# A decoder layer in split float32 on one core: the second norm's rows pipelined on VectorE, three up-projection blocks advancing together over the rows

## The chip, the cores and the metric

One core of a Trainium2 chip runs the kernel: TensorE (PE in the rows) multiplies, VectorE (DVE) and ScalarE (ACT) work element by element, GpSimd (POOL) helps, SyncE (SP) issues the transfers from HBM. The metric is device microseconds of one execution. The times before are the median of 3 runs; the profile is one execution of its own. "Span" is the stretch from the first to the last instruction of that execution.

## What is computed

One layer of a decoder trunk, float32, on 256 positions of 1024 channels. The change lies at the seam of its two halves: the second RMS norm and the ConvFFN behind it.

```
h = rms_norm(x, norm1_g) * (1 + scale1) + shift1
x = x + gate1 * hybrid_token_mixer(h, ...)        # ends in an output projection
h = rms_norm(x, norm2_g) * (1 + scale2) + shift2
u = causal_dwconv(h @ w_up, conv_w, conv_b)       # 1024 -> 2 * 2816, three taps over positions
g, val = split(u, 2)
x = x + gate2 * ((silu(g) * val) @ w_down)        # 2816 -> 1024
```

## The kernel before

**Layout.** Activations are transposed: channels on the 128 partitions, the 256 positions along the free dimension. So the 1024 channels of h are 8 tiles of 128x256, called rows here (`kt` in the code), and a block of 128 output channels is a sum over the 8 rows in half a PSUM bank.

**Split products.** A weight chunk of 128x1024 (512 KB) is split into a rounded part `whi` (L189, ScalarE) and the rest `wlo` (L191, VectorE). An activation is split in the same way, the second norm's h into `h2hi` and `h2lo`. `mm3` (L338 to L340) then gives three matmuls a row: h2hi with whi, h2hi with wlo, h2lo with whi. A block takes 8 rows x 3 = 24 matmuls. A ring of 5 buffers holds split chunks, a ring of 8 the raw ones. SyncE asks for the next raw chunk when its buffer is free (`advance`); `prep` and `get` split ahead of use.

**The second norm (`norm2`, L881).** While the attention part of the output projection ends, the kernel scales each row of x by a gain column `gcol` into `xg` (L870) and sums the squares. The gain is norm2_g (1 + scale2), one 128x1 operation per row (L868). When the sum is there, `rb2` holds 1/rms for each position. Then, for each row, VectorE multiplies y = xg * rb2 into one of three small buffers `hbuf` (L888), ScalarE adds the shift and rounds it into h2hi (L889), and VectorE forms h2lo = y + shift - h2hi (L890). VectorE and ScalarE run this part in the order in which it is written (`manual_schedule`).

**The ConvFFN.** 22 pairs (a gate block and a value block each). Pair 0 is done apart (`up0`): plain float32 matmuls on xg (L919) that don't need the norm, corrected behind it by rb2 (L927, L928). A later pair i is two blocks of 24 matmuls in half-banks of banks 0 to 3 (`up`). Each block gets its convolution: one operation on ScalarE (L903) and two taps on VectorE (L905). The gate goes through Silu (L942, with a load of ScalarE's table the first time), is multiplied by the value (L948), and the product is split (L950, L951). The down-projection (`down`) of pair i - 2 follows pair i; its 8 outputs fill the halves of banks 5, 7, 4 and 6 over all pairs. The order on PE, DVE and ACT outside the norm is set by a scheduler from the program's order and the dependences.

Of the kernel before, what the change touches and what calls it, by code (L numbers as in the profile page):

```python
# [8 lines left out]
F32 = mybir.dt.float32  # L9
F32R = mybir.dt.float32r  # L10
I32 = mybir.dt.int32
AF = mybir.ActivationFunctionType
OP = mybir.AluOpType
AX = mybir.AxisListType

S = 256
D = 1024
KT = D // 128
# [13 lines left out]
V_N2 = 56  # L32
# [15 lines left out]
def mixer_ffn(ctx: ExitStack, tc: tile.TileContext, xT_d, c_d, vec_d, alog_d, ada_d,  # L48
# [7 lines left out]
    act, dve, pool, pe, sp = nc.scalar, nc.vector, nc.gpsimd, nc.tensor, nc.sync  # L56

    def T(shape, name, dt=F32, tag=None):
        return sb.tile(shape, dt, name=name, tag=tag or name)
# [113 lines left out]
    def done(i):  # L173
        freed.add(i)
        advance()
# [20 lines left out]
    def split():  # L196
        for _ in split_steps():
            pass

    def prep(la=LA):  # L200
        while st["split"] < min(st["get"] + 1 + la, NCHUNK):
            split()

    def get(la=LA):
        prep(la)
        i = st["get"]
        st["get"] += 1
        return ready.pop(i)

    cb = T([128, 1024], "cb")  # L210
    vec = T([128, V_ALL], "vec")
    alog = T([128, SH], "alog")
    xT = T([128, KT, S], "xT")
# [17 lines left out]
    mod = T([128, 48], "mod")  # L231
# [20 lines left out]
    def ada_bias(a, b):  # L252
        dve.tensor_tensor(mod[:, a:b], mod[:, a:b], vec[:, V_BADA + a:V_BADA + b], op=OP.add)

    hbuf = Ring(3, [128, S], "hbuf")
# [5 lines left out]
    rb2 = T([128, S], "rb2")  # L261
    acc = T([128, S], "accs")

    def rms_sum(parts, n, pb, between=lambda: None):
        for i, p in enumerate(parts):
            for t in range(2):
                pe.matmul(pb[:, t:t + 1], p[:, t * 128:(t + 1) * 128], ones[:, 0:1], start=(i == t == 0),
                          stop=(i == len(parts) - 1), skip_group_check=True)
        r = rt()
        act.activation(r[:, 2:4], pb[:, 0:2], AF.Sqrt, bias=epsc, scale=1.0 / n)  # L270
        between()
        dve.reciprocal(r[:, 0:2], r[:, 2:4])
        return r
# [15 lines left out]
    def rms_transpose(r, pb):  # L289
        for t in range(2):  # L290
            i = pe.transpose(pb[:, 256 + t * 128:384 + t * 128], r[:, t:t + 1].to_broadcast([128, 128]), ident)
        return i
# [9 lines left out]
    def square_add(i, src, dst, last, late=9):  # L302
        s = dst if i == 0 else sq_r()
        act.activation(s, src, AF.Square)
        if 0 < i < last:
            (dve if i >= late else pool).tensor_tensor(dst, dst, s, op=OP.add)
        return s
# [3 lines left out]
    sc1 = T([128, 2 * KT], "sc1")  # L311
# [25 lines left out]
    def mm3(out, w, h, start, stop):  # L337
        pe.matmul(out, w[0], h[0], start=start, stop=False, skip_group_check=True)  # L338
        pe.matmul(out, w[1], h[0], start=False, stop=False, skip_group_check=True)  # L339
        pe.matmul(out, w[0], h[1], start=False, stop=stop, skip_group_check=True)  # L340

    def sl(w, c):
        return w[0][:, c], w[1][:, c]

    def blk(k):
        return slice(k * 128, k * 128 + 128)


    gcol = T([128, 16], "gcol")
# [4 lines left out]
    def half(b, i):  # L354
        return bank[b][:, i * 256:i * 256 + 256]
# [68 lines left out]
    for kt in range(KT):  # L424
        if kt == 0:
            s1_gain(0)
            s1_h(0)
            ws = [get(0)]
# [15 lines left out]
                                     op0=OP.add, op1=OP.mult)  # L444
            ada_bias(3, 4)
        else:
            s1_mm(kt, [ws[0]], final[:8])
            ws.append(get(0))
            if kt == 2:
# [3 lines left out]
                                         op1=OP.mult)  # L453
# [3 lines left out]
        if kt < KT - 1:  # L457
            s1_h(kt + 1)
            ws = [get(0)]
# [294 lines left out]
    k = P["qk"]  # L754
# [27 lines left out]
    def side(u):  # L782
        for f, a in at.pop(u, []):
            f(*a)
# [3 lines left out]
    for i in range(5):  # L788
        if P["zi"]:
            with tc.issue_after(X["z2"].ins):  # L790
                w = get()
        else:
            w = get()
# [11 lines left out]
    for j in range(6):  # L805
        m, hf = divmod(j, 2)
        bs = (bank[4], bank[6]) if j % 2 else (bank[5], bank[7])
        for q4 in range(4):
            w = get()
            side(5 + 4 * j + q4)  # L810
            c = st["get"] - 1
            for k2 in range(2):
                kt = q4 * 2 + k2 + (m == 2)
# [22 lines left out]
    def aacc(d):  # L836
        return half((0, 1, 5, 4, 6, 7, 2, 3)[d], 0)
# [5 lines left out]
    for d in range(8):  # L843
        w = get()
# [9 lines left out]
    xg = h32  # L854
    for d in range(8):
        w = get()
        if d == 6:
            prep(5)
        side(37 + d)
        for kt in range(8):  # L860
            mm3(aacc(d), sl(w, blk(kt)), (X["ahi"][:, kt], X["alo"][:, kt]), start=(kt == 0), stop=(kt == 7))
        for e in {0: (), 1: (0, 1)}.get(d, (d,)):
            t = hbuf()
            dve.tensor_tensor(t, aacc(e), rb, op=OP.mult)
            dve.scalar_tensor_tensor(xT[:, e], t, gate1(e), xT[:, e], op0=OP.mult, op1=OP.add)
            tail.append(square_add(e, xT[:, e], acc, P['n2l'], P['sqa']))
            g = gcol[:, 8 + e:9 + e]
            dve.scalar_tensor_tensor(g, mod[:, 24 + e:25 + e], sc1[:, KT + e:KT + e + 1], vec[:, V_N2 + e:V_N2 + e + 1],  # L868
                                     op0=OP.add, op1=OP.mult)
            act.activation(xg[:, e, 0:S], xT[:, e], AF.Copy, scale=g)  # L870
        if d == 5:
            tc.keep_in_program_order(act.activation(warm, epsc, AF.Sqrt))
        if d == 6:
            ada_bias(32, 40)
            act.activation(xg[:, :, S:], mod[:, 32:40].unsqueeze(2).to_broadcast([128, KT, 2]), AF.Copy)
    prep()
    assert not at, at
    h2hi = T([128, KT, S], "h2hi", F32R, tag="big_qT")
    h2lo = T([128, KT, S], "h2lo", F32R, tag="big_kT")

    def norm2():  # L881
        r2 = rms_sum([acc] + tail[P['n2l']:], D, bank[5])
        with tc.manual_schedule(engines={mybir.EngineType.DVE, mybir.EngineType.Activation}):
            rms_transpose(r2, bank[5])
            act.activation(rb2, bank[5][:, 256:512], AF.Copy)
            for kt in range(KT):
                y, shift = hbuf(), mod[:, 32 + kt:33 + kt]
                dve.tensor_tensor(y, xg[:, kt, 0:S], rb2, op=OP.mult)  # L888
                act.activation(h2hi[:, kt], y, AF.Identity, bias=shift)  # L889
                dve.scalar_tensor_tensor(h2lo[:, kt], y, shift, h2hi[:, kt].bitcast(F32), op0=OP.add, op1=OP.subtract)  # L890


    fbuf = T([128, 8, S], "fbuf", tag="big_v")
# [7 lines left out]
    def fconv(a, i, src):  # L901
        w = V_FW + 3 * i
        act.activation(a, src, AF.Identity, bias=vec[:, V_FB + i:V_FB + i + 1], scale=vec[:, w + 2:w + 3])  # L903
        for s in (1, 2):
            dve.scalar_tensor_tensor(a[:, s:], src[:, :S - s], vec[:, w + 2 - s:w + 3 - s], a[:, s:],  # L905
                                     op0=OP.mult, op1=OP.add)
# [6 lines left out]
    def up0():  # L913

        ws = get(), get()
        ps = bank[0][:, 0:S + 2], bank[1][:, 0:S + 2]
        for kt in range(KT):
            for p, w in zip(ps, ws):
                pe.matmul(p, w[:, blk(kt)], xg[:, kt], start=(kt == 0), stop=(kt == KT - 1), skip_group_check=True)  # L919
            if kt == P['n2']:  # L920
                norm2()
        for j in (2, 1):
            done(st["get"] - j)
        u = []
        for j in range(2):
            t = hbuf()
            dve.tensor_tensor(t, ps[j][:, 0:S], rb2, op=OP.mult)  # L927
            dve.tensor_scalar(t, t, ps[j][:, S:S + 1], None, op0=OP.add)  # L928
            u.append(t)
        return u  # L930

    def up(i):
        g, v = cg_r(), cv2_r()
        if i == 0:
            pg, pv_ = up0()
        else:
            pg, pv_ = half(2 * i % 4, 0), half((2 * i + 1) % 4, 0)
            w = get()
            for kt in range(KT):
                mm3(pg, sl(w, blk(kt)), (h2hi[:, kt], h2lo[:, kt]), start=(kt == 0), stop=(kt == KT - 1))  # L940
        fconv(g, i, pg)
        act.activation(g, g, AF.Silu)  # L942
        if i:
            w = get()
            for kt in range(KT):
                mm3(pv_, sl(w, blk(kt)), (h2hi[:, kt], h2lo[:, kt]), start=(kt == 0), stop=(kt == KT - 1))
        fconv(v, NF + i, pv_)
        dve.tensor_tensor(v, v, g, op=OP.mult)  # L948
        fh, fl = fhi_r(), flo_r()
        act.activation(fh, v, AF.Copy)  # L950
        dve.tensor_tensor(fl, v, fh.bitcast(F32), op=OP.subtract)  # L951
        return fh, fl

    fs = {}
    for i in range(NF):
        fs[i] = up(i)
        if i >= LAG:
            down(fs.pop(i - LAG), i == LAG)
        if 8 <= i < 16:
            ada_mul(32 + i)  # L960
        if 9 <= i < 17:
            ada_sum(31 + i)
        if i == 17:
            ada_bias(40, 48)
# [3 lines left out]
    ws = [get(), get()]  # L968
# [79 lines left out]
```

## Time and profile before

| what | value |
|---|---|
| median of 3 runs | 437.0 us (436.76 to 437.31) |
| the profiled execution | 437.12 us |
| its span | 435.4 us |
| TensorE busy | 428.0 us (98%) |
| VectorE busy | 338.7 us (78%) |
| ScalarE busy | 259.0 us (59%) |
| GpSimd busy | 34.6 us (8%) |
| granted TensorE clock, mean | 0.996 |

The profiled execution's own time is 1.72 us above its span and 0.12 above the median. In the rows below, times are microseconds from the start of the span unless a column says ns; L888 is line 888 of the kernel before. A matmul's busy time contains the run through the array, which overlaps the next matmul: the pitch between starts is what one costs in a dense stream. PEld are the weight loads of TensorE.

### The profile page before, as it was taken

How to read it: one execution, taken by the hardware profiler on the slowest of the kernel's cores; microseconds unless marked ns; L12 is line 12 of the kernel's file. 1: busy time of each engine (PE TensorE's matmuls, PEld its weight loads, DVE VectorE, ACT ScalarE, POOL GpSimd, SP SyncE). 2: the span in 40 equal slices, each digit the busy share in tenths (PEclk: the TensorE clock that was granted, in tenths of full speed). 3: DMA queues.
4: the chain of work that ended last, by engine and by line, in shares of the span. 5: the costliest groups of instructions: out<-in, count | busy, mean ns of one | idle time of the engine just before them, and what ended most of it. 6: DMA issues, size and time to landing. Idle time of an engine off the chain costs nothing.

```text
span 435.4 us, 7753 instructions
## 1 busy us (share of the span) xinstructions
PE 428.0 (98%) x2952; PEld 387.7 (89%) x2952; DVE 338.7 (78%) x670; ACT 259.0 (59%) x513; POOL 34.6 (8%) x31
## 2 busy tenths in 40 slices
PE   8999999999999999999999899999999999999996
PEld 9799998768766668888999699999999999999996
DVE  2779968999788998668699489787877876776655
ACT  4365448826998965642258386567766655555540
POOL 2000000000000020201220000032233200000000
PEclk9899999999999999999999999999999999999999
DMA  7999964899277644057790527866776565454002
GB/s 283 400 415 408 394 200 172 306 325 336 74 279 276 219 164 176 17 201 250 294 390 11 230 109 240 296 239 202 278 255 233 204 219 184 169 193 147 2 2 96
DMA packets 29589, 96.71 MB, mean 222 GB/s; under 512 B 3552, under 2 KB 6000, under 8 KB 29552
## 3 DMA queue, kind: packets, MB, share of 16 engines
q1 hardware_dynamic: 29520, 96.20, 61.1%
q8 instruction: 23, 0.38, 0.4%
q14 instruction: 14, 0.11, 0.1%
q10 hardware_dynamic: 32, 0.02, 0.0%
HBM read 95.14 MB, written 1.06 MB: 221 GB/s over the span
## 4 chain that ended last, share of the span: by engine, by line
PE 84%; DVE 7%; ACT 5%; issue 1%; DMA 1%; POOL 1%; ACTq 0%; POOLq 0%
PE bank L338 15%; PE bank L339 15%; PE bank L340 15%; PE bank L847 6%; PE bank L798 4%; PE bank L819 4%; PE bank L821 4%; PE bank L823 3%; PE bank L822 3%; DVE adax L239 2%; PE bank L412 2%; PE bank L228 2%; ACT whi L189 2%; DVE wlo L191 2%; PE bank L919 1%
## 5 line engine op out<-in xcount | busy, mean ns | idle before, releaser
L191 DVE TENSOR_TENSOR wlo<-raw,whi 128x1024 fp32r<-128x1024 f32 (+2 forms) x107 | 132.8, 1242 | 17.8 <-ACT whi L189 17.7
L189 ACT ACTIVATE whi<-raw 128x1024 fp32r<-128x1024 f32 (+2 forms) x106 | 108.6, 1032 | 39.8 <-PE bank L340 23.7
L338 PE MATMUL bank<-h2hi,whi 128*128 128x256 f32 x336 | 95.4, 285 | 2.1 <-ACT h2hi L889 1.9
L339 PE MATMUL bank<-h2hi,wlo 128*128 128x256 f32 x336 | 94.5, 283 | 0.0
L340 PE MATMUL bank<-h2lo,whi 128*128 128x256 f32 x336 | 93.9, 284 | 0.0
L338 PEld LDWEIGHTS bank<-h2hi,whi 128*128 128x128 f32 x336 | 64.4, 192 | 3.7 <-ACT h2hi L889 3.2
L339 PEld LDWEIGHTS bank<-h2hi,wlo 128*128 128x128 f32 x336 | 64.4, 192 | 0.0
L340 PEld LDWEIGHTS bank<-h2lo,whi 128*128 128x128 f32 x336 | 63.8, 192 | 0.2 <-DVE h2lo L890 0.2
L905 DVE SCALAR_TENSOR_TENSOR fbuf<-bank,vec,fbuf 128x255 f32<-128x255 f32 x84 | 40.3, 481 | 29.4 <-ACT fbuf L903 28.1
L244 POOL TENSOR_TENSOR ada<-ada,cb 128x1024 f32<-128x1024 f32 x11 | 28.8, 2621 | 270.2 <-DMA ada<-in_ada_dram 270.2
L338 PE MATMUL bank<-fsp,whi 128*128 128x256 f32 x176 | 49.8, 284 | 0.0
L339 PE MATMUL bank<-fsp,wlo 128*128 128x256 f32 x176 | 49.7, 283 | 0.0
L340 PE MATMUL bank<-fsp,whi 128*128 128x256 f32 x176 | 49.6, 283 | 0.0
L903 ACT ACTIVATE fbuf<-bank,vec 128x256 f32<-128x256 f32 x42 | 23.4, 560 | 36.2 <-PE bank L340 36.2
L239 DVE SCALAR_TENSOR_TENSOR ada<-ada,cb 128x1024 f32<-128x1024 f32 x27 | 32.8, 1216 | 3.0 <-DMA ada<-in_ada_dram 3.0
L338 PEld LDWEIGHTS bank<-fsp,whi 128*128 128x128 f32 x176 | 33.8, 192 | 0.1
L339 PEld LDWEIGHTS bank<-fsp,wlo 128*128 128x128 f32 x176 | 33.8, 192 | 0.0
L340 PEld LDWEIGHTS bank<-fsp,whi 128*128 128x128 f32 x176 | 33.7, 192 | 0.0
L821 PE MATMUL bank<-whi,hhi 128*128 128x512 f32 x70 | 29.5, 422 | 0.0
L847 PE MATMUL bank<-y,raw 128*128 128x256 f32 x128 | 28.9, 380 | 0.0
L822 PE MATMUL bank<-wlo,hhi 128*128 128x512 f32 x70 | 28.6, 408 | 0.0
L823 PE MATMUL bank<-whi,hlo 128*128 128x512 f32 x70 | 28.3, 405 | 0.0
(214 smaller groups left out, 783.1 us busy)
## 6 DMA issues: line engine op xcount, KB each, us to landing
raw<-in_wup_dram SPq DMA_DIRECT2D x44, 512.0 KB, 4.1
ada<-in_ada_dram SPq DMA_DIRECT2D x38, 512.0 KB, 5.1
raw<-in_wdn_dram SPq DMA_DIRECT2D x22, 512.0 KB, 3.6
raw<-in_winq_dram SPq DMA_DIRECT2D x16, 512.0 KB, 4.8
raw<-in_wout_dram SPq DMA_DIRECT2D x16, 512.0 KB, 3.8
adax<-in_ada_dram SPq DMA_DIRECT2D x10, 512.0 KB, 9.6
raw<-in_win_dram SPq DMA_DIRECT2D x8, 456.0 KB, 9.7
raw<-in_win_dram SPq DMA_DIRECT2D x7, 512.0 KB, 9.8
```

What stands on the lines that cost most here:

```text
L189: act.activation(hi[:, c], t[:, c], AF.Copy)
L191: (pool if lo_on_pool(i) else dve).tensor_tensor(lo[:, c], t[:, c], hi[:, c].bitcast(F32), op=OP.subtract)
L239: dve.scalar_tensor_tensor(t, t, 1.0, sc, op0=OP.mult, op1=OP.mult, accum_out=mod[:, i:i + 1])
L244: pool.tensor_tensor(adas[i], adas[i], sc, op=OP.mult)
L338: pe.matmul(out, w[0], h[0], start=start, stop=False, skip_group_check=True)
L339: pe.matmul(out, w[1], h[0], start=False, stop=False, skip_group_check=True)
L340: pe.matmul(out, w[0], h[1], start=False, stop=stop, skip_group_check=True)
L821: pe.matmul(bs[t], hhi[:, kt, blk(t)], w[0][:, wc], start=(q4 == k2 == 0), stop=False)
L822: pe.matmul(bs[t], hhi[:, kt, blk(t)], w[1][:, wc], start=False, stop=False)
L823: pe.matmul(bs[t], hlo[:, kt, blk(t)], w[0][:, wc], start=False, stop=(kt == KT - 1))
L847: pe.matmul(sacc(d), w[:, blk(kt)], X["y32"][:, kt], start=(kt == d % 2 == 0), stop=(kt == 7), skip_group_check=True)
L905: dve.scalar_tensor_tensor(a[:, s:], src[:, :S - s], vec[:, w + 2 - s:w + 3 - s], a[:, s:], op0=OP.mult, op1=OP.add)
```

## The change

Three edits. The gain columns of all 8 rows are formed by two 128x8 operations at the start of the attention output projection's loop, where a 128x1 operation per row stood in the loop. In the norm, y of the next row is written ahead of h2lo of the row before. In `up`, the value block of pair 1 and the gate block of pair 2 are fetched together with the gate block of pair 1, and all three take a row before any takes the next; the gate block of pair 2 sums in bank 6 (it was bank 0). A call of `prep()` is added in `up0`.

```diff
         side(37 + d)
+        if d == 0:
+            g = gcol[:, 8:16]
+            dve.tensor_tensor(g, mod[:, 24:32], sc1[:, KT:], op=OP.add)
+            dve.tensor_tensor(g, g, vec[:, V_N2:V_N2 + 8], op=OP.mult)
...
-            g = gcol[:, 8 + e:9 + e]
-            dve.scalar_tensor_tensor(g, mod[:, 24 + e:25 + e], sc1[:, KT + e:KT + e + 1], vec[:, V_N2 + e:V_N2 + e + 1],
-                                     op0=OP.add, op1=OP.mult)
-            act.activation(xg[:, e, 0:S], xT[:, e], AF.Copy, scale=g)
+            act.activation(xg[:, e, 0:S], xT[:, e], AF.Copy, scale=gcol[:, 8 + e:9 + e])
...
-            for kt in range(KT):
-                y, shift = hbuf(), mod[:, 32 + kt:33 + kt]
-                dve.tensor_tensor(y, xg[:, kt, 0:S], rb2, op=OP.mult)
-                act.activation(h2hi[:, kt], y, AF.Identity, bias=shift)
-                dve.scalar_tensor_tensor(h2lo[:, kt], y, shift, h2hi[:, kt].bitcast(F32), op0=OP.add, op1=OP.subtract)
+            ys = {}
+            for kt in range(KT + 1):
+                if kt < KT:
+                    ys[kt] = hbuf()
+                    dve.tensor_tensor(ys[kt], xg[:, kt, 0:S], rb2, op=OP.mult)
+                    act.activation(h2hi[:, kt], ys[kt], AF.Identity, bias=mod[:, 32 + kt:33 + kt])
+                if kt:
+                    k = kt - 1
+                    dve.scalar_tensor_tensor(h2lo[:, k], ys.pop(k), mod[:, 32 + k:33 + k], h2hi[:, k].bitcast(F32),
+                                             op0=OP.add, op1=OP.subtract)
...
         ws = get(), get()
+        prep()
...
-            w = get()
+            if i == 2:
+                pg = half(6, 0)
+            ws = [] if i == 2 else [(pg, get())]
+            if i == 1:
+                ws += [(pv_, get()), (half(6, 0), get())]
             for kt in range(KT):
-                mm3(pg, sl(w, blk(kt)), (h2hi[:, kt], h2lo[:, kt]), start=(kt == 0), stop=(kt == KT - 1))
+                for p, w in ws:
+                    mm3(p, sl(w, blk(kt)), (h2hi[:, kt], h2lo[:, kt]), start=(kt == 0), stop=(kt == KT - 1))
         fconv(g, i, pg)
         act.activation(g, g, AF.Silu)
-        if i:
+        if i > 1:
             w = get()
```

VectorE's order in the norm, before (L888 is y, L890 is h2lo; hbuf_163 to hbuf_165 are the three buffers):

```order
L272 RECIPROCAL rt_173<-rt_173 128x2
L888 TENSOR_TENSOR hbuf_164<-h_168,rb_175 128x256
L890 SCALAR_TENSOR_TENSOR h2lo<-hbuf_164,mod,h2hi 128x256
L888 TENSOR_TENSOR hbuf_165<-h_168,rb_175 128x256
L890 SCALAR_TENSOR_TENSOR h2lo<-hbuf_165,mod,h2hi 128x256
L888 TENSOR_TENSOR hbuf_163<-h_168,rb_175 128x256
L890 SCALAR_TENSOR_TENSOR h2lo<-hbuf_163,mod,h2hi 128x256
```

The same place in the changed kernel (L891 is y, L895 is h2lo):

```order
L272 RECIPROCAL rt_173<-rt_173 128x2
L891 TENSOR_TENSOR hbuf_164<-h_168,rb_175 128x256
L891 TENSOR_TENSOR hbuf_165<-h_168,rb_175 128x256
L895 SCALAR_TENSOR_TENSOR h2lo<-hbuf_164,mod,h2hi 128x256
L891 TENSOR_TENSOR hbuf_163<-h_168,rb_175 128x256
L895 SCALAR_TENSOR_TENSOR h2lo<-hbuf_165,mod,h2hi 128x256
L891 TENSOR_TENSOR hbuf_164<-h_168,rb_175 128x256
L895 SCALAR_TENSOR_TENSOR h2lo<-hbuf_163,mod,h2hi 128x256
```

One y now stands between a row's y and its h2lo.

TensorE's order over rows 0 and 1, as a difference (bank_67 is bank 2 with pair 1's gate block, bank_68 bank 3 with its value block, bank_71 bank 6 with pair 2's gate block):

```order
 L339 MATMUL bank_68<-h2hi,wlo_89 128x256
 L340 MATMUL bank_68<-h2lo,whi_84 128x256
+L338 MATMUL bank_71<-h2hi,whi_85 128x256
+L339 MATMUL bank_71<-h2hi,wlo_90 128x256
+L340 MATMUL bank_71<-h2lo,whi_85 128x256
 L338 MATMUL bank_67<-h2hi,whi_83 128x256
 L339 MATMUL bank_67<-h2hi,wlo_88 128x256
+L340 MATMUL bank_67<-h2lo,whi_83 128x256
 L338 MATMUL bank_68<-h2hi,whi_84 128x256
 L339 MATMUL bank_68<-h2hi,wlo_89 128x256
-L340 MATMUL bank_67<-h2lo,whi_83 128x256
 L340 MATMUL bank_68<-h2lo,whi_84 128x256
```

Before, a row was 6 matmuls, the two with h2lo last; now it is 9, each block's three together.

ScalarE's order behind the rows in the changed kernel (L909 convolution, L954 Silu with its table load, L962 the rounded product, L189 the split of the next weights; bank_71 is bank 6):

```order
L909 ACTIVATE fbuf<-hbuf_163,vec 128x256
L909 ACTIVATE fbuf<-hbuf_164,vec 128x256
L954 ACT_TABLE_LOAD
L954 ACTIVATE fbuf<-fbuf 128x256
L909 ACTIVATE fbuf<-bank_67,vec 128x256
L909 ACTIVATE fbuf<-bank_68,vec 128x256
L962 ACTIVATE fsp<-fbuf 128x256
L909 ACTIVATE fbuf<-bank_71,vec 128x256
L189 ACTIVATE whi_83<-raw_78 128x1024
```

Before, pair 0's gate convolution stood ahead of the last row's h2hi, and that of bank_67 ahead of the table load.

## Rows read from the trace of the kernel before

**Rows 1.** The page, busy time of TensorE.
```profile
PE 428.0 (98%) x2952; PEld 387.7 (89%) x2952; DVE 338.7 (78%) x670; ACT 259.0 (59%) x513; POOL 34.6 (8%) x31
```

**Rows 2.** Stage windows: length, busy (x) PE PEld DVE ACT POOL, PEclk, DMA share, GB/s.
```profile
242.70:252.00 9.30, 7.28 (x45) 5.80 (x44) 6.35 (x17) 3.66 (x8) 0.00 (x0) 1.00 0.88 343
...
259.00:345.00 86.00, 86.00 (x717) 85.98 (x717) 70.72 (x96) 57.44 (x88) 19.91 (x8) 1.00 0.72 245
345.00:432.00 87.00, 86.95 (x725) 86.75 (x723) 61.67 (x98) 44.26 (x67) 0.00 (x0) 1.00 0.37 122
```

**Rows 3.** Chain of waits, row 0 of the norm: start, length on the chain, what.
```profile
241.74 0.44 DVE hbuf L888
242.20 0.52 ACT h2hi L889
242.74 0.48 DVE h2lo L890
```

**Rows 4.** Timeline of VectorE: start, us, instruction [idle before <- releaser].
```profile
243.14 0.41 DVE L888 TENSOR_TENSOR hbuf<-h,rb 128x256 f32<-128x256 f32 x1
...
250.12 0.42 DVE L888 TENSOR_TENSOR hbuf<-h,rb 128x256 f32<-128x256 f32 x1
250.45 0.42 DVE L927 TENSOR_TENSOR hbuf<-bank,rb 128x256 f32<-128x256 f32 x1
250.91 0.36 DVE L928 TENSOR_SCALAR hbuf<-hbuf,bank 128x256 f32<-128x256 f32 x1
251.18 0.48 DVE L890 SCALAR_TENSOR_TENSOR h2lo<-hbuf,mod,h2hi 128x256 fp32r<-128x256 f32 x1
...
252.64 0.48 DVE L890 SCALAR_TENSOR_TENSOR h2lo<-hbuf,mod,h2hi 128x256 fp32r<-128x256 f32 x1
...
254.31 1.00 DVE L905 SCALAR_TENSOR_TENSOR fbuf<-bank,vec,fbuf 128x255 f32<-128x255 f32 x2 [0.54 <-ACT fbuf L903]
...
260.07 1.21 DVE L191 TENSOR_TENSOR wlo<-raw,whi 128x1024 fp32r<-128x1024 f32 x1
```

**Rows 5.** Waits from 242 to 259 us: who, for whom, us, times, longest.
```profile
PEld bank L338 <- ACT h2hi L889: 3.2, 6, 0.6
```

**Rows 6.** Timeline of TensorE, row 0 and the end of pair 2.
```profile
242.76 0.39 PE L338 MATMUL bank<-h2hi,whi 128*128 128x256 f32 x1
...
243.28 0.39 PE L340 MATMUL bank<-h2lo,whi 128*128 128x256 f32 x1
243.50 0.28 PE L338 MATMUL bank<-h2hi,whi 128*128 128x256 f32 x1
...
258.31 0.28 PE L340 MATMUL bank<-h2lo,whi 128*128 128x256 f32 x1
258.71 0.38 PE L338 MATMUL bank<-h2hi,whi 128*128 128x256 f32 x1
259.02 0.39 PE L338 MATMUL bank<-fsp,whi 128*128 128x256 f32 x1
```

**Rows 7.** Timeline of ScalarE behind the rows.
```profile
254.29 1.28 ACT L942 ACT_TABLE_LOAD   x1
255.59 0.42 ACT L942 ACTIVATE fbuf<-fbuf 128x256 f32<-128x256 f32 x1
255.91 0.59 ACT L903 ACTIVATE fbuf<-hbuf,vec 128x256 f32<-128x256 f32 x1
...
256.71 1.00 ACT L903 ACTIVATE fbuf<-bank,vec 128x256 f32<-128x256 f32 x2
257.61 1.05 ACT L189 ACTIVATE whi<-raw 128x1024 fp32r<-128x1024 f32 x1
```

**Rows 8.** Timeline of SyncE's queue: issues of weight transfers.
```profile
226.07 16.88 SPq L146 DMA_DIRECT2D raw<-in_wup_dram  x2
```

**Rows 9.** The gain columns and the nearest 128x8 operation: ns min/median/max, first and last start.
```profile
L868 DVE SCALAR_TENSOR_TENSOR gcol<-mod,sc,vec x8: 209/214/215, 111.8 to 162.2; 128x1 f32<-128x1 f32 x8
L253 DVE TENSOR_TENSOR mod<-mod,vec x11: 150/151/160, 12.6 to 346.7; 128x1 f32<-128x1 f32 x8, 128x8 f32<-128x8 f32 x3
```

## The prediction

> **What bounds the kernel now.** The busy times come first: TensorE is busy for 428.0 of 435.4 us, so only a place where it idles, or where its stream gets longer, can move the time [rows 1]. The stage windows say where that is. From 242.70 to 252.00 it is busy for 7.28 of 9.30 us, with 45 matmuls; from 259 to 345 for all 86.00, with 717 matmuls, so one each 0.120 us; from 345 to 432 for 86.95 of 87 [rows 2]. The granted clock is 1.00 in all three, so the level is 2.4 GHz throughout and no clock is to be won. The chain of waits shows what the first of these stretches waits for: VectorE's product y (L888), ScalarE's rounding h2hi (L889), VectorE's rest h2lo (L890), and only then the next y [rows 3]. VectorE issues the next y 0.40 us behind the h2lo (242.74 to 243.14), so one of the 8 rows takes 243.14 - 241.74 = 1.40 us [rows 3, 4]. In it TensorE has 6 matmuls, 0.72 us. The weight loads wait 3.2 us for h2hi [rows 5].
>
> How much is lost is read from TensorE's timeline. The four blocks of pairs 1 and 2 are 4 x 24 = 96 matmuls, 11.52 us at 0.120. The first starts at 242.76; the last starts at 258.31 and frees the array at 258.43. That is 15.67 us, so 4.15 are idle. Then two gaps follow: one matmul of pair 3 at 258.71, and the down-projection of pair 0 at 259.02 [rows 6]. Its place in a dense stream would be 259.02 - 0.12 = 258.90.
>
> **The rows, new order.** VectorE runs y0, y1, h2lo0, y2, h2lo1 and so on. A y costs it 0.33 to 0.34 us (250.12 to 250.45), an h2lo 0.40 [rows 3, 4]. The first h2lo can't come sooner: y0 at 241.74, h2hi at 242.20, h2lo at 242.74, as now, with y1 in the gap. From then on h2hi of the next row is ready in time: y(k+1) starts 0.74 us ahead of its h2lo or more, and ScalarE's 0.46 + 0.52 + 0.02 us on the chain overlap one further VectorE pair. So h2lo(k) starts at 242.74 + 0.74k, and row 7 at 247.92, done at 248.40 (0.48 each). Three buffers are enough: y(k+3) overwrites what h2lo(k) has read two instructions ahead. Before, row 7's h2lo starts at 252.64, 9.9 us behind row 0's; now it would be 5.2 us behind it [rows 4].
>
> **Three blocks over the rows.** TensorE gets 9 matmuls a row, 1.08 us, against 0.74 us for a row on VectorE: it becomes the slower of the two and stays dense. Row 0 keeps its stall: two matmuls at 242.76, the third, which needs h2lo, at 243.28, the next at 243.50 [rows 6]. The other 69 of the 72 follow at 0.120: 243.50 + 8.28 = 251.78. The up block of pair 2's value half (24, weights split ahead of the norm) ends at 254.66. So the down-projection starts 258.90 - 254.66 = **4.24 us** sooner. Of 4.15 + 0.47 us of gaps only row 0's 0.38 is left. With the pipelined rows alone, two blocks would have 0.72 us of matmuls a row against 0.74, almost the same; the third block is mainly cover for a late row.
>
> **What must be ready by then.** I follow VectorE and ScalarE behind the rows in the changed order.
> - Pair 0's product. Its four operations on VectorE start at 247.58 (ahead of h2lo7), 248.32, 248.59 and 249.05: 0.34 + 0.40 with h2lo7 between, then 0.27, then 0.46 for one that needs the result before it [rows 4]. ScalarE's convolution of the gate, 0.59, begins when the second is done; the gate's two taps follow at 249.35 and end at 250.35, 1.00 for two [rows 4, 7]. The table load stands behind them: 250.39 to 251.67; Silu 251.69 to 252.11; the product at 252.14 [rows 7]. Meanwhile ScalarE takes the convolutions of banks 2 and 3, 252.01 and 252.45, then the rounded product, 252.90 to 253.31. VectorE's rest comes behind two taps, at 253.43, and ends at 253.85. TensorE needs it for its third matmul, 254.66 + 0.24 = 254.90. Margin 1.05.
> - Bank 6. The third block accumulates there, and the seventh output of the down-projection overwrites it, 18 matmuls in, at 256.82. Its second tap sits behind pair 1's product, that behind Silu, that behind the split of pair 3's weights on ScalarE (0.96 us on the chain at 253.65, 1.05 by itself [rows 7]). It ends at 255.88. Margin 0.94.
> - Pair 3's weights. VectorE's part follows that tap: 255.80 to 257.01 at 1.21 [rows 4]. TensorE's second matmul of pair 3 needs it at 257.66. Margin 0.65, the thinnest. The raw weights were asked for at 226.07 [rows 8].
>
> So I cost the tail at nothing, under the cover of 48 matmuls (5.76 us); if it comes L later, TensorE loses L - 0.65.
>
> The table load took 1.28 us at 254.29 and the next Silu started at 255.59, 1.30 us later: nothing else stands there [rows 7]. The Trainium skill says otherwise (ScalarE: Activation LUTs, What ACT_TABLE_LOAD costs): a switch is the 1283 ns load and about 1380 ns of drain. By that rule the rest of pair 0 would end at 255.23 and cost 0.33, the weights would be another 0.40 late, and the sum would be 3.51 rather than 4.24. The trace disagrees with it here, so the sum keeps the row.
>
> **gcol and prep.** Eight 128x1 operations of 0.21 us at 111.8 to 162.2 go; two 128x8 ones come, 0.15 by the nearest row [rows 9]. Seven of the eight stand between the dependent steps of a reciprocal square root while TensorE is dense, and the two new ones stand there too: I take zero, between a loss of 0.3 (two, if something waited for them) and a gain of 1.7 (eight, if VectorE bound there). The added prep() issues nothing: the splits stand at the same places in the order. No DMA is added; SP's order is unchanged, and transfers are let go by buffers that TensorE's stream frees, so they move with it.
>
> **Sum.** 4.24 us off the profiled execution's 437.12 is 432.9; off the median, 437.0, 432.8. I take **432.8**. From 259 on TensorE never waits, so nothing downstream takes it back by slack.
>
> **Rivals.**
> 1. The tail becomes the bound. For it: margins of 0.65 to 1.05 us rest on some 20 modelled starts. One more piece as long as the table load's 1.28 would cost 1.28 - 0.65 = 0.63, a loss of the same size as the skill's rule gives; 433.4, or up to 434.5 if it is late by 2.3. Chance 0.10.
> 2. The rows don't overlap (a buffer of the ring released late). With 1.40 us a row, TensorE has 1.08 in it; row 7's h2lo is usable at 253.18, its 7 last matmuls end near 254.1, pair 2's value half at 257.0: gain 1.9, 435.1. Against: the order is as told, and the ring's waits are on instructions long done. Chance 0.04.
> 3. Given back later: the weight stream can't come 4 us sooner. For it: the DMA share is 0.72 in 259 to 345 [rows 2]. Against: TensorE didn't wait there once. 437.0, no change. Chance 0.04.
> 4. Slower: bank 6. If the split of pair 3's weights waits for its transfer, Silu, pair 1's product and the tap queue behind it, and TensorE stops in the middle of the down-projection, where before the third block had bank 0. It decides when the transfer lands after 253.65; slower than before it gets where that is over 0.94 + 4.24 = 5.2 us later, past 258.8. At 6 us late it gives 437.0 + 0.8 = 437.8. Against: 27 us of lead [rows 8]. Chance 0.02.
>
> **Numbers.** The forecast has 0.80. The least the time can be is all gaps gone, 0.38 more, 432.4; with the 0.24 by which the lowest run lies under the median, 432.1. The upper end takes rival 1 at a delay of 2 us: 434.2. Faster by over 0.2% (about what a measurement of this kernel can tell from no change): 0.80 + 0.10 + 0.04 = 0.94; within: 0.04; slower: 0.02.
>
> **What would show it.** TensorE's timeline: no idle entry between 243.5 and the end, its down-projection first at about 254.7, nine matmuls each 1.08 us. VectorE: y and h2lo in turn at 0.74 us, no idle entry on h2hi behind the first. ScalarE: its idle entries before h2hi gone. The span is 431.2. Wrong: an idle entry on TensorE for the rounded product, for bank 6's tap or for the weights of pair 3 (rival 1 or 4), rows still at 1.40 (rival 2), or idle entries past 259 (rival 3).

## The result, and the profile after

The changed kernel takes **432.92 us** (median of 6 runs, 432.34 to 434.12), the kernel before 437.06 in the same comparison (6 runs, 436.43 to 437.31). The ratio is 0.9915, with a 95% interval of 0.9904 to 0.9926: faster by 4.1 us. The forecast was 432.8 in a range of 432.1 to 434.2. The profiled execution took 432.34, with a span of 430.6.

The page's busy times of the changed kernel answer to [rows 1]:

```profile
PE 425.2 (99%) x2952; PEld 386.7 (90%) x2952; DVE 339.6 (79%) x664; ACT 258.9 (60%) x513; POOL 34.1 (8%) x31
```

The same 2952 matmuls are in the profile. VectorE has 6 instructions fewer (eight gain columns out, two in). The stage windows of the changed kernel, with the columns of [rows 2], say where the time came from:

```profile
242.70:252.00 9.30, 9.29 (x77) 9.20 (x77) 8.28 (x23) 6.37 (x12) 0.00 (x0) 1.00 0.93 352
252.00:259.00 7.00, 7.00 (x61) 7.00 (x60) 6.95 (x15) 7.00 (x13) 0.00 (x0) 1.00 0.35 122
259.00:345.00 86.00, 86.00 (x719) 86.00 (x718) 72.61 (x95) 56.67 (x88) 19.85 (x8) 1.00 0.73 246
```

In the first stretch 77 matmuls run where 45 ran [rows 2]; 9.30 us at 0.120 is 77.5, so it is dense. From 259 to 345 nothing has changed: 719 matmuls for 717, DMA share 0.73 for 0.72. Nothing was given back there.

VectorE's timeline in the changed kernel (L891 is y, L895 is h2lo, L963 the rest of a pair's product, L911 a convolution tap, L191 VectorE's part of a weight split; "x2" is two records in one row):

```profile
241.27 0.76 DVE L891 TENSOR_TENSOR hbuf<-h,rb 128x256 f32<-128x256 f32 x2 [1.15 <-ACT rb L886]
242.27 0.48 DVE L895 SCALAR_TENSOR_TENSOR h2lo<-hbuf,mod,h2hi 128x256 fp32r<-128x256 f32 x1 [0.24 <-ACT h2hi L892]
242.67 0.42 DVE L891 TENSOR_TENSOR hbuf<-h,rb 128x256 f32<-128x256 f32 x1
243.00 0.48 DVE L895 SCALAR_TENSOR_TENSOR h2lo<-hbuf,mod,h2hi 128x256 fp32r<-128x256 f32 x1
...
247.39 0.47 DVE L895 SCALAR_TENSOR_TENSOR h2lo<-hbuf,mod,h2hi 128x256 fp32r<-128x256 f32 x1
...
252.94 0.41 DVE L963 TENSOR_TENSOR fsp<-fbuf,fsp 128x256 fp32r<-128x256 f32 x1
...
254.90 0.47 DVE L911 SCALAR_TENSOR_TENSOR fbuf<-bank,vec,fbuf 128x254 f32<-128x254 f32 x1
255.29 1.22 DVE L191 TENSOR_TENSOR wlo<-raw,whi 128x1024 fp32r<-128x1024 f32 x1
```

Two y's run ahead of the first h2lo; from then on they take turns, one row in 243.00 - 242.27 = 0.73 us where it was 1.40. Row 7's h2lo starts 247.39 - 242.27 = 5.12 us behind row 0's, where it was 9.9 [rows 4]. The idle entry of 0.24 for h2hi is the only one of its kind.

TensorE's timeline, row 0 and the end of the three blocks, answers to [rows 6]:

```profile
242.29 0.39 PE L338 MATMUL bank<-h2hi,whi 128*128 128x256 f32 x1
242.51 0.28 PE L339 MATMUL bank<-h2hi,wlo 128*128 128x256 f32 x1
242.81 0.39 PE L340 MATMUL bank<-h2lo,whi 128*128 128x256 f32 x1
243.03 0.28 PE L338 MATMUL bank<-h2hi,whi 128*128 128x256 f32 x1
...
254.19 0.28 PE L338 MATMUL bank<-fsp,whi 128*128 128x256 f32 x1
...
254.43 0.28 PE L340 MATMUL bank<-fsp,whi 128*128 128x256 f32 x1
...
257.07 0.28 PE L338 MATMUL bank<-h2hi,whi 128*128 128x256 f32 x1
257.19 0.28 PE L339 MATMUL bank<-h2hi,wlo 128*128 128x256 f32 x1
```

Row 0 still has its stall (242.51 to 242.81). The down-projection starts at 254.19, 11.90 us behind the first matmul of the rows; before it was 259.02 - 242.76 = 16.26, of which 0.12 is the one matmul of pair 3 that stood ahead of it [rows 6]. All waits of the weight loads between 241 and 262 us come to one row of the view of waits, and ScalarE's for y to another:

```profile
ACT h2hi L892 <- DVE hbuf L891: 2.1, 7, 0.5
...
PEld bank L340 <- DVE h2lo L895: 0.2, 1, 0.2
```

The 3.2 us for h2hi [rows 5] are gone.

**A measure that is free of what lies ahead.** In the profiled executions shown here the first matmul of the rows starts anywhere from 242.18 to 243.10, whatever the kernel, before any of this seam has run. So I compare executions by the *stretch* from that matmul to the start of the kernel's last matmul. Before: 431.68 - 242.76 = 188.92. After: 426.87 - 242.29 = 184.58, which is **4.34 shorter**. The span shrank by 435.4 - 430.6 = 4.8; the other 0.47 is where the rows began, 242.29 for 242.76, and is not owed to the change by anything seen here: with the new gain columns the rows begin at 242.18 to 243.10 in seven executions, with the old ones at 242.24 to 242.97 in three.

### The profile page after: what moved, and what is told of

It is laid out like the page before. It is cut to its first block, busy times and chain, and to the rows that moved or that the text cites. A ratio compares the mean times of both kernels' runs of the same rounds, so it can differ in the third digit from the quotient of the medians.

```text
span 430.6 us, 7750 instructions
## 1 busy us (share of the span) xinstructions
PE 425.2 (99%) x2952; PEld 386.7 (90%) x2952; DVE 339.6 (79%) x664; ACT 258.9 (60%) x513; POOL 34.1 (8%) x31
## 4 chain that ended last, share of the span: by engine, by line
PE 87%; DVE 6%; ACT 3%; DMA 1%; issue 1%; POOL 1%; ACTq 0%; POOLq 0%
PE bank L340 16%; PE bank L338 16%; PE bank L339 16%; PE bank L847 6%; PE bank L798 4%; PE bank L819 4%; PE bank L821 4%; PE bank L823 3%; PE bank L822 3%; DVE adax L239 2%; PE bank L412 2%; PE bank L228 2%; PE bank L926 2%; DVE wlo L191 2%; ACT whi L189 1%; DMA ada<-in_ada_dram 1%
## 5 line engine op out<-in xcount | busy, mean ns | idle before, releaser
L191 DVE TENSOR_TENSOR wlo<-raw,whi 128x1024 fp32r<-128x1024 f32 (+2 forms) x107 | 133.1, 1245 | 18.7 <-ACT whi L189 18.7
L189 ACT ACTIVATE whi<-raw 128x1024 fp32r<-128x1024 f32 (+2 forms) x106 | 108.5, 1032 | 40.3 <-PE bank L340 23.6
L340 PE MATMUL bank<-h2lo,whi 128*128 128x256 f32 x336 | 95.2, 283 | 0.0
L911 DVE SCALAR_TENSOR_TENSOR fbuf<-bank,vec,fbuf 128x255 f32<-128x255 f32 (+1 forms) x84 | 40.2, 481 | 26.8 <-ACT fbuf L909 25.5
L909 ACT ACTIVATE fbuf<-bank,vec 128x256 f32<-128x256 f32 x42 | 23.5, 561 | 33.9 <-PE bank L340 33.9
```

What stands on the lines that cost most here:

```text
L189: act.activation(hi[:, c], t[:, c], AF.Copy)
L191: (pool if lo_on_pool(i) else dve).tensor_tensor(lo[:, c], t[:, c], hi[:, c].bitcast(F32), op=OP.subtract)
```

## The experiments

The theory: the time comes from VectorE's serial row alone; TensorE was short of rows, and the third block covers a late row but earns little; everything behind the rows has 0.65 us or more to spare. The rivals: the third block is what pays (more work per row, so that 1.40 us hide); the new tail is what bounds; the gain columns have a share.

**The changed kernel once more**, with no edit, on the chip of the next three kernels, beside 17 runs of the kernel before (437.15, 436.21 to 438.09).

> The changed kernel once more, as the yardstick for the runs beside it. Theory (rows and blocks keep TensorE dense from row 0 on): 4.2 us under the kernel before, one stall of 0.3 us on the first h2lo, no idle entry later. Rival (the gain is that of one chip): less than 3.5 us.

Measured: 432.91 (4 runs, 432.38 to 433.22), ratio 0.9902, interval 0.9887 to 0.9916; stretch 426.91 - 242.33 = 184.58, as in the first profile. The gain stands on a second comparison, and the stretch repeats to 0.01 us.

**Pipelined rows alone.** The gain columns, `up` and `prep()` are as before; the edit to the changed kernel, cut:

```diff
-            if i == 2:
-                pg = half(6, 0)
-            ws = [] if i == 2 else [(pg, get())]
-            if i == 1:
-                ws += [(pv_, get()), (half(6, 0), get())]
+            w = get()
             for kt in range(KT):
-                for p, w in ws:
-                    mm3(p, sl(w, blk(kt)), ...)
+                mm3(pg, sl(w, blk(kt)), ...)
...
-        if i > 1:
+        if i:
```

> The rows pipelined on VectorE, nothing else. Theory (the serial row of 1.40 us was the loss; two blocks have 0.72 us of matmuls against a row of 0.74): 3.6 to 4.2 us under the kernel before, with idle entries of TensorE in the rows of 0.5 us at most together, and up to 0.4 us for pair 0's product, since ScalarE here splits the next weights ahead of the table load. Rival (the third block is what keeps TensorE busy): a gain under 2 us, with idle entries on h2hi or h2lo in every row.

Measured: 432.90 (4 runs, 432.35 to 433.33), ratio 0.9902, interval 0.9887 to 0.9917; stretch 427.76 - 242.97 = 184.79, so 4.13 of the 4.34 us. TensorE's timeline of this kernel, rows 0 and 1 and the start of the down-projection:

```profile
242.97 0.39 PE L338 MATMUL bank<-h2hi,whi 128*128 128x256 f32 x1
...
244.06 0.28 PE L339 MATMUL bank<-h2hi,wlo 128*128 128x256 f32 x1
244.22 0.39 PE L340 MATMUL bank<-h2lo,whi 128*128 128x256 f32 x1
244.44 0.30 PE L338 MATMUL bank<-h2hi,whi 128*128 128x256 f32 x1
...
255.08 0.28 PE L338 MATMUL bank<-fsp,whi 128*128 128x256 f32 x1
```

With six matmuls a row TensorE is about as fast as VectorE and runs into row 1 before its h2lo is there: the next matmul comes 0.16 behind 244.06 where 0.12 is the pitch, and the one after that 0.22. The down-projection starts 12.11 us behind the first matmul, for 11.90 in the change. That is the 0.21 us by which the third block shortens the stretch; the timed medians can't tell the two kernels apart.

**Three blocks alone.** The changed kernel with the norm's loop as it was:

```diff
-            ys = {}
-            for kt in range(KT + 1):
...
+            for kt in range(KT):
+                y, shift = hbuf(), mod[:, 32 + kt:33 + kt]
+                dve.tensor_tensor(y, xg[:, kt, 0:S], rb2, op=OP.mult)
+                act.activation(h2hi[:, kt], y, AF.Identity, bias=shift)
+                dve.scalar_tensor_tensor(h2lo[:, kt], y, shift, h2hi[:, kt].bitcast(F32), ...)
```

> Three blocks over the rows, the rows serial as before (gcol and prep as in the change). Theory: a row stays at 1.40 us, TensorE has 1.08 us of matmuls in it, pair 2's value half would end 1.9 us sooner, and the tail behind the rows (pair 0's product, the next weights) costs 0.3 to 0.8 of that: 1.1 to 1.9 us under the kernel before. Rival (the third block carries the gain): 3 us or more.

Measured: 435.81 (12 runs, 434.96 to 436.76), ratio 0.997, interval 0.9959 to 0.9981; stretch 429.88 - 242.27 = 187.61, so 1.31 shorter than before. The waits of its weight loads from 241 to 262 us:

```profile
PEld bank L338 <- ACT h2hi L890: 1.4, 5, 0.3
PEld bank L338 <- ACT fsp L957: 0.4, 1, 0.4
PEld bank L339 <- DVE wlo L191: 0.2, 1, 0.2
PEld bank L338 <- DVE fbuf L906: 0.2, 1, 0.2
...
```

A row of 1.40 us with 1.08 us of matmuls leaves TensorE waiting for h2hi, as before but less: 1.4 us for 3.2. And since the rows end late, what follows them is late too: waits for pair 0's product, pair 3's weights and a tap appear, which the changed kernel has not. The two edits aren't parts of a sum (4.13 + 1.31 is more than 4.34); they remove the same idle time, and the rows remove nearly all of it alone.

**Row 0's stall taken away.** In row 0 of the three blocks the six matmuls that need only h2hi go ahead of the three that need h2lo:

```diff
             for kt in range(KT):
+                if i == 1 and kt == 0:
+                    for p, w in ws:
+                        for j in range(2):
+                            pe.matmul(p, w[j][:, blk(0)], h2hi[:, 0], start=(j == 0), ...)
+                    for p, w in ws:
+                        pe.matmul(p, w[0][:, blk(0)], h2lo[:, 0], start=False, ...)
+                    continue
```

> The changed kernel, and in row 0 the six matmuls with h2hi of all three blocks stand ahead of the three with h2lo. Theory: the one stall left, 0.30 us on the first h2lo, is filled: the down-projection of pair 0 starts 0.28 to 0.38 us sooner behind the first row's matmul than in the change, time 0.3 us under it (too little for the timing alone). Rival (the tail's margin of 0.65 us is used up elsewhere): the stall turns up again as a wait for pair 3's weights.

Measured: 432.5 (4 runs, 432.35 to 432.58), ratio 0.9893, interval 0.988 to 0.9906; stretch 427.09 - 242.79 = 184.30, 0.28 shorter than the change. TensorE's timeline of this kernel (L954 are the six, L956 the three):

```profile
242.79 0.39 PE L954 MATMUL bank<-h2hi,whi 128*128 128x256 f32 x1
243.02 0.28 PE L954 MATMUL bank<-h2hi,wlo 128*128 128x256 f32 x1
...
243.61 0.52 PE L956 MATMUL bank<-h2lo,whi 128*128 128x256 f32 x3
...
254.41 0.28 PE L338 MATMUL bank<-fsp,whi 128*128 128x256 f32 x1
...
257.41 0.28 PE L339 MATMUL bank<-h2hi,wlo 128*128 128x256 f32 x1
```

No wait of a weight load is left in the seam, and the down-projection starts 254.41 - 242.79 = 11.62 us behind the first matmul, 0.28 sooner than in the change. It is the fastest kernel of this study by the profile; the two timed medians, 432.5 and 432.91, have ranges that overlap, so the timing alone doesn't settle 0.28 us. The price is margin: VectorE's part of pair 3's weights ends at 257.02 in this kernel and is needed at 257.41, 0.39 us to spare for 0.68.

**A late row, with and without the third block.** Two extra 128x512 copies on ScalarE, whose result nobody reads, stand ahead of row 4's h2hi. One kernel adds them to the pipelined rows alone, the other to the changed kernel:

```diff
             for kt in range(KT + 1):
+                if kt == 4:
+                    for _ in range(2):
+                        act.activation(junk, sc[:, 0:512], AF.Copy)
                 if kt < KT:
```

> Only the rows pipelined (two blocks), and two idle 128x512 copies on ScalarE between h2hi of rows 3 and 4: 1.06 us of work, of which 0.22 fits into ScalarE's gap, so rows 4 to 7 come 0.84 us late. Theory (two blocks keep pace with the rows and have no lead): TensorE idles 0.7 to 0.85 us at row 4, and from the first matmul of the rows to the last of the kernel it takes 185.5 to 185.7 us, against 184.79 without the copies. Rival (the weights split ahead give a lead here too): under 0.3 us lost.

Measured, rows alone with the copies: 433.19 in one run, stretch 427.75 - 242.24 = 185.51, so 0.72 longer than the rows alone without them. Row 4's h2hi comes 0.87 us late. First ScalarE's timeline of this kernel, then TensorE's:

```profile
244.22 1.28 ACT L892 ACTIVATE junk<-cb 128x512 f32<-128x512 f32 x2
245.41 0.89 ACT L896 ACTIVATE h2hi<-hbuf,mod 128x256 fp32r<-128x256 f32 x2
```

```profile
245.55 0.28 PE L340 MATMUL bank<-h2lo,whi 128*128 128x256 f32 x1
245.95 0.38 PE L338 MATMUL bank<-h2hi,whi 128*128 128x256 f32 x1
246.18 0.28 PE L339 MATMUL bank<-h2hi,wlo 128*128 128x256 f32 x1
...
255.62 0.28 PE L339 MATMUL bank<-h2hi,wlo 128*128 128x256 f32 x1
255.84 0.39 PE L338 MATMUL bank<-fsp,whi 128*128 128x256 f32 x1
256.06 0.28 PE L339 MATMUL bank<-fsp,wlo 128*128 128x256 f32 x1
```

TensorE stops for the late row: 0.40 us from 245.55 to 245.95 where 0.12 is the pitch, and 0.23 to the next, so 0.39 beyond the pitch. That is about half of the 0.7 to 0.85 us that the theory put here. It took two blocks to have no lead, but ScalarE makes h2hi a row ahead of h2lo. In the rows alone without the copies, row 4's h2hi ends at 245.27 + 0.51 = 245.78, 0.51 us ahead of its first matmul. ScalarE's timeline of that kernel, then TensorE's:

```profile
245.27 0.51 ACT L891 ACTIVATE h2hi<-hbuf,mod 128x256 fp32r<-128x256 f32 x1 [0.22 <-DVE hbuf L890]
```

```profile
246.29 0.29 PE L338 MATMUL bank<-h2hi,whi 128*128 128x256 f32 x1
```

So about 0.4 of the 0.87 reaches TensorE, an estimate from these rows, and the scheduler fills 0.12 of it with one more matmul with h2lo. Further 0.20 go where the down-projection begins (0.22 twice, for 0.12), since pair 0's product is late. The late row alone doesn't make it so: with the copies in the program the scheduler put one more split of weights ahead of it on ScalarE, and its rounded half starts 255.38 - 242.24 = 13.14 us behind the first matmul, for 254.20 - 242.97 = 11.23 without the copies. That the total fell into the forecast range is therefore in part luck: the loss lies in other places than forecast.

> The changed kernel (three blocks) with the same two copies at the same place. Theory (9 matmuls a row, 1.08 us against 0.73, give a lead of some 1.5 us by row 4): no idle entry in the rows; only the tail is 0.84 late, which costs 0.84 - 0.65 = 0.2 us at pair 3's weights; 184.6 to 184.9 us from the first matmul of the rows to the last, against 184.58. Rival (no cover from the third block): 0.7 us or more lost, at row 4.

Measured, the change with the copies: 432.35 in one run, stretch 426.89 - 242.18 = 184.71, 0.13 longer than the change. There is no wait in the rows but row 0's. What is left comes from the tail. VectorE's timeline of this kernel shows its part of pair 3's weights:

```profile
255.97 1.22 DVE L191 TENSOR_TENSOR wlo<-raw,whi 128x1024 fp32r<-128x1024 f32 x1
```

It ends at 257.19, 15.01 us behind the first matmul; in the change it ends 255.29 + 1.22 - 242.29 = 14.22 behind it. It is 0.79 late with 0.68 to spare, which makes 0.11; 0.13 was lost. TensorE's timeline shows that the sum comes out so well by terms that nearly cancel:

```profile
256.99 0.40 PE L338 MATMUL bank<-h2hi,whi 128*128 128x256 f32 x2
257.24 0.39 PE L339 MATMUL bank<-h2hi,wlo 128*128 128x256 f32 x1
257.47 0.28 PE L340 MATMUL bank<-h2lo,whi 128*128 128x256 f32 x1
```

The scheduler put a second matmul with h2hi ahead of the one that takes wlo (in the change there is one), which adds 0.12 to the margin. The operand is taken 0.05 behind its end, and the matmul behind that one comes at 0.23, not 0.12. So 0.79 - 0.68 - 0.12 + 0.05 + 0.11 = 0.15, for 0.13; TensorE hardly idles here, and most of the loss is the late pitch. The third block covers the late row itself in full: nothing is lost in the rows, where 0.39 was without it. The totals, 0.13 and 0.72, also contain two tails that the scheduler ordered differently, so their difference is not all owed to the third block.

**A late tail.** Seven such copies behind the last h2hi in the changed kernel; the scheduler spreads them over ScalarE's tail:

```diff
+            for _ in range(7):
+                act.activation(junk, sc[:, 0:512], AF.Copy)
```

> The changed kernel with seven idle 128x512 copies on ScalarE behind the last h2hi, which the order spreads over the tail (before pair 0's convolutions, before the table load, and behind the first Silu); the split of pair 3's weights starts L later behind the first matmul of the rows than the 10.87 us of the change, and L should be 2.0 to 2.9. Theory (margin 0.65 at pair 3's weights): TensorE loses L - 0.65, 1.3 to 2.2 us, at the down-projection of pair 0 or at pair 3's weights. Rival (the margin is larger, the chain isn't the next bound): under 0.8 us lost.

Measured: 434.52 in one run, stretch 429.06 - 243.10 = 185.96, 1.38 longer than the change. The waits of the weight loads:

```profile
PEld bank L338 <- ACT whi L189: 0.6, 2, 0.3
PEld bank L339 <- DVE wlo L191: 0.2, 1, 0.2
...
PEld bank L338 <- DVE fbuf L915: 0.2, 1, 0.2
```

TensorE waits for both parts of pair 3's weights and for a tap. The wait for VectorE's part ends last. VectorE's timeline, then TensorE's:

```profile
258.12 1.22 DVE L191 TENSOR_TENSOR wlo<-raw,whi 128x1024 fp32r<-128x1024 f32 x1
```

```profile
259.40 0.39 PE L339 MATMUL bank<-h2hi,wlo 128*128 128x256 f32 x1
259.62 0.28 PE L340 MATMUL bank<-h2lo,whi 128*128 128x256 f32 x1
```

That part ends at 259.34, 16.24 us behind the first matmul, so 2.02 late. Behind 259.62 TensorE's stream is dense again, so this last wait sets the loss and contains the ones ahead of it. 2.02 less the margin of 0.68 is 1.34, against 1.38 measured; with the three terms of the late row, 2.02 - 0.68 - 0.12 + 0.06 + 0.10 = 1.38. This is worked out from the result. The rule as it was put on record takes the delay of ScalarE's part, which starts 13.37 behind the first matmul for 10.87 in the change: 2.50 late, so 1.85 lost, 0.47 too much. VectorE made up part of that: it took up its part 258.12 - (256.47 + 1.05) = 0.60 us behind ScalarE's end, where it was 255.29 - (253.16 + 1.05) = 1.08 in the change.

**The gain columns and prep() alone**, on the kernel before:

```diff
+        if d == 0:
+            g = gcol[:, 8:16]
+            dve.tensor_tensor(g, mod[:, 24:32], sc1[:, KT:], op=OP.add)
+            dve.tensor_tensor(g, g, vec[:, V_N2:V_N2 + 8], op=OP.mult)
...
-            g = gcol[:, 8 + e:9 + e]
-            dve.scalar_tensor_tensor(g, mod[:, 24 + e:25 + e], ...)
...
         ws = get(), get()
+        prep()
```

> Only the two 128x8 operations for the eight 128x1 ones, and the added prep. Theory: nothing, 188.9 us from the first matmul of the rows to the last, as before, and no new wait. Rival (VectorE's 1.7 us count, or prep moves a split): more than 0.3 us either way.

Measured: 436.69 in one run, beside one of the kernel before at 436.79; stretch 431.24 - 242.33 = 188.91 for 188.92. The two new operations take 156 and 161 ns. The longest of TensorE's waits between 241 and 262 us in it:

```profile
PEld bank L338 <- ACT h2hi L890: 3.2, 6, 0.6
```

The seam is that of the kernel before, down to the 3.2 us [rows 5]. This edit lies ahead of the stretch, and the time doesn't show it either: nothing, within what one run and a start of the rows that scatters by 0.9 us can tell.

## Why the prediction was right

**What bounded.** Right: TensorE waited on VectorE's serial row. Pipelined rows alone give 4.13 of 4.34 us, and three blocks over serial rows only 1.31.

**The row.** 0.74 us was forecast, 0.73 measured; row 7's h2lo was to come 5.2 us behind row 0's and comes 5.12 behind. One of the signs named was wrong: ScalarE's idle entries ahead of h2hi did not go. It still waits for y seven times, 2.1 us in all, because VectorE gives one y in 0.73 us and an h2hi takes 0.52. TensorE has no wait for h2hi: the one it takes was made earlier.

**The 4.24 us.** The down-projection was to start 254.66 - 242.76 = 11.90 us behind the first matmul of the rows, with row 0's stall kept. It starts 254.19 - 242.29 = 11.90 behind it. The stretch shrank by 4.34, 0.10 more than the sum. That 0.10 is the kernel before's second restart: behind 259.02 its next matmul had a pitch of 0.22, and the sum had counted the idle time up to 259.02 alone. The span was to be 431.2 and is 430.6; 0.47 of that is the earlier start of the rows. The medians give 437.06 - 432.92 = 4.14 and 437.15 - 432.91 = 4.24. That the median came within 0.12 of the forecast is in part luck, since single runs of the changed kernel lie up to 1.8 us apart; the stretch is the sharper test.

**The margins.** This was the long part of the working, and it holds row by row. Pair 0's rest ends at 252.94 + 0.41 = 253.35 and its matmul is at 254.43: 1.08 for 1.05 forecast. Bank 6's second tap ends at 254.90 + 0.47 = 255.37; the matmul that overwrites it, 18 behind 254.19, is at 256.35: 0.98 for 0.94. Pair 3's weights end at 256.51 and are needed at 257.19: 0.68 for 0.65. That the loss is the delay less this margin was only argued. With the delay of VectorE's part, the operand whose wait ends last, the two kernels with extra copies come to it within 0.05 us (0.13 for 0.11, 1.38 for 1.34), but only because an added matmul, the time from an operand's end to its matmul and the late pitch behind a wait nearly cancel. With the delay of ScalarE's split, as the rule was applied ahead of the run, it gives 1.85 for 1.38.

**The table load.** ScalarE's timeline of the changed kernel:

```profile
249.89 1.28 ACT L954 ACT_TABLE_LOAD   x1 [0.39 <-DVE fbuf L911]
251.18 0.42 ACT L954 ACTIVATE fbuf<-fbuf 128x256 f32<-128x256 f32 x1
```

Silu starts 1.29 us behind the load's start, as the row of before had it (1.30, [rows 7]); the load itself starts 7.60 us behind the first matmul for 7.63 forecast. The Trainium skill (ScalarE: Activation LUTs, What ACT_TABLE_LOAD costs) has about 1380 ns of drain beside the 1283 ns of the load. The 1283 agrees with the row; the drain stands nowhere in it, and the 0.73 us by which the prediction's estimate by that page was lower were not lost.

**The rivals.** Tail: its margins weren't used up (rival 1), and it does bind once it is made late: 2.02 us late, it cost 1.38. Rows that don't overlap: at 0.73 us they do; the nearest kernel, three blocks over serial rows, took 435.81 for the 435.1 of rival 2, because the late tail, which that rival left out, came on top. Given back later: 719 matmuls in 86.00 us. Bank 6: no wait for it. That the third block would cover a late row, and that on top of the pipelined rows it would earn almost nothing, were both forecast; the first is shown by one run of each kernel, the second by 0.21 us. That two blocks cover nothing of a late h2hi, as the theory of that run had it, was wrong: they covered about half.

## What to carry to other kernels

Where three steps on two engines make a row, and the row bounds, write the first step of row k+1 ahead of the last of row k: here that was worth 4.13 us, and giving the starved engine half as much work again per row only 1.31. Make the sum on the starved engine's timeline, and then follow each later operand to the moment it is needed: the seam moves 4 us ahead of them all, and the smallest margin, here 0.68 us, says about how much of a disturbance is still free. If the first row has a bubble, put what needs only the early operand first: one reordered row took away the last wait.

## What the runs showed beside this

**Busy time hid half of the stall.** The window of the kernel before over the rows and the rest of pair 2 reads:

```profile
242.70:259.00 16.30, 14.15 (x99) 12.37 (x97) 11.52 (x30) 9.43 (x19) 0.00 (x0) 1.00 0.58 226
```

By busy time 16.30 - 14.15 = 2.15 us were idle. By count 99 matmuls at 0.120 are 11.88 us, so 4.42 were lost: a matmul that starts behind a gap is booked with up to 0.39 us of busy time for 0.28, and with gaps between matmuls their booked times no longer overlap. That is also most of why the page's busy TensorE fell from 428.0 to 425.2 with the same 2952 matmuls: 14.15 - 11.88 = 2.27 of the 2.8 us lie here, and the rest ahead of the rows, which began 0.47 earlier. The prediction's 4.15 us came from counting matmuls, and a sum from the share of idle time would have come to half.

**A restart costs a pitch.** A matmul that comes behind a stall and is booked with 0.38 or 0.39 us is followed at 0.21 us or more in every trace here, mostly at 0.22, not at 0.12 (242.81 to 243.03 after; 245.95 to 246.18 with the late row), with the granted clock at 1.00 in these windows. Even a stall of 0.01 us ended so (257.24 to 257.47). Some short stalls cost less: the matmul at 244.44 in the rows alone is booked with 0.30, and the next came 0.15 behind it. What takes this time no run shows. So each wait of the first kind costs about 0.10 us more than its idle time; the six waits of [rows 5] come to some 0.6 us in this way, an estimate from that pitch.
